# A fifth tile pair for FFN 1's second product, and residual weight parts added up by transfers

## The chip, the cores and the metric

One core of one Trainium2 chip runs the whole layer as one program. The metric is device microseconds (us) of one execution. Five engines take part, each with its own in-order instruction stream: PE (matmul), DVE (elementwise work), ACT (activation, copies), POOL (here mostly the issuer of some transfers) and SP (the issuer of most transfers). They meet through semaphores. Transfers (DMA) run on 16 DMA engines; those issued by SP appear in the profile as queue q1, those issued by POOL as queue q0.

## The reference

A layer of a streaming encoder on 512 tokens of width 1024, all in float32:

```
f = (silu(n1(x) @ w1) * (n1(x) @ w3)) @ w2          # FFN 1, D_FF = 2816 = 22 tiles of 128
h = x + 0.5 * post1(f)
... input projection, recurrent branch, windowed attention, gates, w_o: h = h + post_mix(...)
f = (silu(n2(h) @ w1') * (n2(h) @ w3')) @ w2'        # FFN 2, the same shapes
y = h + 0.5 * post2(f)
```

n1, n2 and the posts are RMS norms with a gain. The change touches the two FFNs alone.

## The kernel before

**Split operands.** Every float32 matmul is made of three: an operand is split into a high part (ACT copies it to the matmul's rounded type, `whi`) and a low part (DVE subtracts: `wlo = raw - whi`), and PE adds hi·hi, lo·hi and hi·lo. So each 128x1024 weight tile costs one ACT copy and one DVE subtraction before PE can use it.

**Pair jobs.** In the FFNs' first products (w1 and w3) two neighbouring hidden tiles make a job that needs seven quarter products in place of eight (Winograd's form of Strassen's scheme). `Pairs.run` goes through 16 such jobs for FFN 1 (hidden tiles 6 to 21, w1 and w3 in turn, two raw tiles `ra` and `rb` each) and 18 for FFN 2. The PE order in a job is: a11, s1, then the last product (a22) of the job before, then s2, a12, s4, s3. Each is one `mm_s`: four steps of three 128x256 matmuls, and ends with `point()`. While job n runs, `Pairs.prep(n + 1, i)` makes the operands of the next: i = 0 the sums S12 and S34 (DVE), i = 1 the split of `ra` (it gives a11 and a12; its low part is the `wlo<-raw_w1a` and `wlo<-raw_w3a` of the traces), i = 2 and 3 the splits of the sums, i = 4 the split of a22. ACT also copies the finished products out of PSUM in each job (q1 after a11, q5 after s1, u after s2).

**`later` and `point`.** `later(n, fn, rank)` puts work off until n calls of `point()` on; each PE product calls it. So the order on ACT, DVE, SP and POOL is set by counts of products.

**The w2 product** (`w2_gemm`) goes through 22 hidden tiles. In FFN 1 (`w2a`), `W2["w2a"] = (6, (4,), 6, 0.95)`: six tiles in the plain form, then one group of four tile pairs (tiles 6 to 13), in the form with seven products for eight, then tiles 14 and 15 plain, then the last six tiles token tile by token tile in `tok_finish`, where the norm and the residual follow. A plan sorted by due times spreads the splits and sums of all tiles ahead of PE. For FFN 2's w2 the weight parts of five pairs are made far ahead by `pre_pair` and stored in DRAM (`PRE`, `PRE_AT`); `w_load` brings them back.

**Slots.** All tiles of 128x1024 floats share 43 slots of SBUF; a load into a slot waits for the last reader of what lay there.

Of the kernel before, what the change touches and what calls it, by code (L numbers as in the profile page):

```python
# [11 lines left out]
F32R = mybir.dt.float32r  # L12
AF = mybir.ActivationFunctionType
ALU = mybir.AluOpType

P = 128
SEQ = 512
D = 1024
# [33 lines left out]
def hybrid_layer(ctx: ExitStack, tc: tile.TileContext, a: dict, out: bass.AP):  # L52
# [126 lines left out]
    def later(n, fn, rank=1):  # L179
        uid[0] += 1  # L180
        due.append((now[0] + n, rank, uid[0], fn))
# [29 lines left out]
    def unit(nm, i, **kw):  # L211
        w = get(nm, i)
        ps = bank("f")
        mm_feat(ps, w, **kw)
        return ps
# [218 lines left out]
    def pre_pair(nm, f, at0, step):  # L434
        made = PRE_TILES.setdefault(nm, {})
        dram = [tc.dram_tile([P, D], F32, name=f"pre_{nm}{f}_{i}") for i in range(5)]
        made[f] = [dram[:2], *dram[2:]]
        r, t = [], {}

        def load():  # L440
            for n in range(2):
                r.append(slot([P, D], name="rawp"))
                src = a[nm][f * P : (f + 2) * P, n * 512 : n * 512 + 512]
                sp.dma_start(out=r[n].rearrange("p (b c) -> p b c", b=2), in_=src.rearrange("(b p) c -> p b c", p=P))

        def hi(name, src, w=QH):
            if w == D:
                t[name] = slot([P, D], F32R, name="ph"), slot([P, D], F32R, name="pl")
            else:
                x = slot([P, 2, QH], F32R, name="pb")  # L450
                t[name] = x[:, 0, :], x[:, 1, :], x
            t[name] = *t[name], src
            act.activation(t[name][0], src, AF.Copy)

        def lo(name):
            x = t[name]
            dve.tensor_tensor(out=x[1], in0=x[-1], in1=f32(x[0]), op=ALU.subtract)

        def store(i, name):
            x = t.pop(name)  # L460
            if i == 0:
                for d, y in zip(dram[:2], x):
                    sp.dma_start(out=d, in_=f32(y))
            else:
                sp.dma_start(out=dram[i + 1], in_=f32(x[2].rearrange("p a b -> p (a b)")))

        def sums34():
            t34_of(*r)
            hi("t3", r[1][:, :QH])

        steps = [
            (load,),
            (),
            (lambda: hi("t12", t12_of(*r), D),),
            (lambda: lo("t12"), lambda: hi("b22", r[1][:, QH:])),
            (lambda: store(0, "t12"), lambda: lo("b22")),
            (sums34, lambda: store(1, "b22")),
            (lambda: lo("t3"), lambda: hi("t4", r[0][:, QH:])),
            (lambda: store(2, "t3"), lambda: lo("t4"), lambda: r.clear()),
            (lambda: store(3, "t4"),),  # L480
        ]
        for i, fns in enumerate(steps):
            later(at0 + i * step, lambda fns=fns: [fn() for fn in fns], 4)

    def pre_at(where):
        for nm, f, at_, step in PRE_AT.get(where, ()):
# [349 lines left out]
    QH = 4 * P  # L836
# [13 lines left out]
    class Pairs:  # L850
# [13 lines left out]
        def prep(self, m, i):  # L864
            if m >= len(self.jobs):
                return
            k = self.k0 + 2 * m
            if i == 0:
                if k not in loaded or k + 1 not in loaded:
                    self.raws(m)  # L870
                s12, s34 = slot([P, 2 * QH], name="S12"), slot([P, 2 * QH], name="S34")
                self.w[m] = {"r": (raws.pop(k), raws.pop(k + 1)), "s": (s12, s34)}
            W = self.w[m]
            (ra, rb), (s12, s34) = W["r"], W["s"]
            a11, a12, a21, a22 = ra[:, :QH], ra[:, QH:], rb[:, :QH], rb[:, QH:]

            def both(src, w=2 * QH):
                hi = slot([P, w], F32R, name="whi")
                lo = slot([P, w], F32R, name="wlo")
                split2(hi, lo, src)  # L880
                return hi, lo

            def halves(p, a, b):
                W[a] = p[0][:, :QH], p[1][:, :QH]
                W[b] = p[0][:, QH:], p[1][:, QH:]

            if i == 0:
                dve.tensor_tensor(out=s12[:, :QH], in0=a21, in1=a22, op=ALU.add)
                dve.tensor_tensor(out=s12[:, QH:], in0=s12[:, :QH], in1=a11, op=ALU.subtract)
                dve.tensor_tensor(out=s34[:, QH:], in0=a12, in1=s12[:, QH:], op=ALU.subtract)  # L890
                dve.tensor_tensor(out=s34[:, :QH], in0=a11, in1=a21, op=ALU.subtract)
            elif i == 1:
                halves(both(ra), "a11", "a12")
            elif i == 2:
                halves(both(s12), "s1", "s2")
            elif i == 3:
                halves(both(s34), "s3", "s4")
            elif i == 4:
                t = slot([P, 2, QH], F32R, name="w22")
                split2(t[:, 0, :], t[:, 1, :], a22)  # L900
                W["a22"] = t[:, 0, :], t[:, 1, :]
                del W["r"], W["s"]

        def run(self, tail, hooks={}):
# [4 lines left out]
            for n, (nm, f) in enumerate(self.jobs):  # L909
                W = self.w.pop(n)  # L910
# [7 lines left out]
                at = lambda i: [f() for f in hooks.get((n, i), ())]  # L918
                mm_s(W["a11"], X["b11"], bu)
                act.activation(q1, bu, AF.Copy)  # L920
                if n == len(self.jobs) - 1:
                    tail()
                at(1)
                mm_s(W["s1"], X["t1"], bx)
                act.activation(q5, bx, AF.Copy)
                at(2)
                last()
                self.prep(n + 1, 1)
                mm_s(W["s2"], X["t2"], bu, True)
                del W["s1"], W["s2"]  # L930
                act.activation(u, bu, AF.Copy)
# [53 lines left out]
    def load_x(k, q=sp):  # L985
        q.dma_start(out=xts[k // 2][:, k % 2, :], in_=a["xT"][k * P : (k + 1) * P, :])

    def load_w(u, kp):
        nm, i = order[u]
        c = slice(kp * 2 * P, (kp + 1) * 2 * P)  # L990
        sp.dma_start(out=raw3[u][:, c], in_=a[nm][i * P : (i + 1) * P, c])


    warm = slot([P, 512], F32R, name="warm")
# [3 lines left out]
        pe.matmul(psw, warm[:, :P], warm, start=True, stop=True)  # L998

    load_x(0, act)  # L1000
    sp.dma_start(out=vec, in_=a["vec"])
    for kp in range(KT // 2):
        load_w(0, kp)
        if kp:
            load_x(2 * kp)
        load_w(1, kp)
        load_w(2, kp)
        load_x(2 * kp + 1)
    dma_to(NS + 2)
# [54 lines left out]
    pairs_a.prep(0, 0)  # L1064
    ps.append(unit("w3a", 1))
    pairs_a.prep(0, 1)
    p1 = unit("w1a", 2)
    pairs_a.prep(0, 2)

# [19 lines left out]
    def softplus(at0, at1):  # L1089
        lam = vec[:, V_LAM : V_LAM + KT]  # L1090
        z = [small(KT, "z", 5) for _ in range(5)]

        def heads():
            act.activation(z[0], lam, AF.Abs)
            act.activation(z[1], z[0], AF.Exp, scale=-1.0)

        steps = []

        def tt(o, x, y):
            steps.append(lambda: dve.tensor_tensor(out=o, in0=x, in1=y, op=ALU.mult))  # L1100

        def ts(o, x, s1, s2, op0, op1=None):
            kw = {"op1": op1} if op1 else {}
            steps.append(lambda: dve.tensor_scalar(out=o, in0=x, scalar1=s1, scalar2=s2, op0=op0, **kw))

        ts(z[2], z[1], 2.0, None, ALU.add)
        steps.append(lambda: dve.reciprocal(z[2], z[2]))
        tt(z[1], z[1], z[2])
        tt(z[2], z[1], z[1])
        ts(z[3], z[2], 1.0 / 17, 1.0 / 15, ALU.mult, ALU.add)  # L1110
        for c in (13, 11, 9, 7, 5, 3, 1):
            tt(z[3], z[3], z[2])
            ts(z[3], z[3], 1.0 / c, None, ALU.add)
        tt(z[3], z[3], z[1])
        ts(z[4], lam, -1.0, 0.0, ALU.mult, ALU.max)
        steps.append(lambda: dve.scalar_tensor_tensor(out=z[3], in0=z[3], scalar=2.0, in1=z[4], op0=ALU.mult, op1=ALU.add))
        ts(chalf, z[3], 2.0, None, ALU.mult)
        ts(cneg, z[3], -4.0, None, ALU.mult)
        ts(bhalf, vec[:, V_BA : V_BG + 16], 0.5, None, ALU.mult)
        later(at0, heads)  # L1120
        for i, step in enumerate(steps):
            later(at1 + i, step, 4)
# [66 lines left out]
        split_to(st["split"] + 1)  # L1189

    softplus(6, 9)
    pairs_a.run(w2_ahead, late)
    X1 = pairs_a = late = None
    bs = w2_gemm("w2a", hid, "ffn1_post_g", 0.5, "mix_pre_g", [("xr", i) for i in range(4)], x_t, h1)
# [352 lines left out]
        later(2 + i, lambda i=i: X2.update({f"t{i + 1}": to_slots(tn[i])}))  # L1547
    pairs_b = Pairs("w1b", "w3b", NC2, X2, hid)
    end = 2 * 2 * (NC2 - 2)
    for i, at_ in enumerate((end - 7, end - 4, end - 3, end - 2, end - 1)):  # L1550
        later(at_, lambda i=i: pairs_b.prep(0, i))
    later(end, lambda: pairs_b.prep(1, 0))
    swiglu_units("w1b", "w3b", 2, NC2, hid)
# [17 lines left out]
SCAN_LAG = (1, 2, 3, 4, 6, 7, 9, 10)  # L1571
NSLOT = 43
RO = 6
W2 = {"w2a": (6, (4,), 6, 0.95), "w2b": (2, (4, 4), 4, 0.95)}
TR_K = {"w2a": 2, "wo": 4}
PRE = {"w2b": (2, 4, 6, 8, 14)}
PRE_AT = {"xr": [("w2b", 2, 2, 2), ("w2b", 8, 8, 2)], "xg": [("w2b", 4, 7, 1)], ("wg", 13): [("w2b", 6, 1, 1)], "wao": [("w2b", 14, 4, 1)]}
W2_LOAD = (14, 9, 8, 8)
P0A, P0B = 6, 8
W2_LEAD = 2.5  # L1580
W2_RAW = 4
W2_FLUSH = 2.5
# [57 lines left out]
```

## Time and profile before

| | |
|---|---|
| median of 3 runs | 1120.33 us (1120.18 to 1120.45) |
| profiled execution | 1120.09 us, its span 1118.3 us |
| granted TensorE clock | 0.999 |
| busy | PE 99%, DVE 81%, ACT 54%, POOL 3% of the span |
| FFN 1 pair jobs | 72.4 to 233.7 us of the span |
| FFN 1 w2, plain tiles 0 to 5 | 233.7 to 266.7 us |
| group of four pairs | 266.7 to 304.8 us |
| tiles 14 and 15 | 304.8 to 315.4 us |

The 1.8 us between span and time lie around the program. The chain of waits that ended last runs over PE for 98% of the span. Matmul records overlap, since PE is pipelined: what a matmul costs is the distance from its start to the next one's.

### The profile page before, as it was taken

The page shows a single profiled execution, that of the slowest core. Times are in us where ns is not written, and L with a number is a line of the kernel's source. Part 1 is how long each engine was busy: PE and PEld are TensorE (multiplying, and loading weights), DVE is VectorE, ACT ScalarE, POOL GpSimd, SP SyncE. Part 2 cuts the span into 40 slices and gives each one's busy share as a digit, 9 for nine tenths or more (in the row PEclk, how much of TensorE's full clock was granted, in tenths as well). Part 3 has the DMA queues.
Part 4 walks back from the last instruction along what each step waited for, and adds up shares of the span by engine and source line. Part 5 has one row for each costly group of instructions (what it writes and reads, how often), then busy time and mean ns, then how long its engine had stood idle before and what let it go on. Part 6 is the DMA issues. An engine that isn't in the chain of part 4 may idle for free.

```text
span 1118.3 us, 17215 instructions
## 1 busy us (share of the span) xinstructions
PE 1109.7 (99%) x6613; PEld 987.7 (88%) x6613; DVE 907.3 (81%) x1609; ACT 607.8 (54%) x1072; POOL 34.7 (3%) x60
## 2 busy tenths in 40 slices
PE   9999999999999999999999999999999999999997
PEld 7889999988889887888888888888999999998886
DVE  5999888888887777886799877777868888887995
ACT  7555555564455368945655664355644555555352
POOL 0000000000000000001021111000000000000000
PEclk9999999999999999999999999999999999999999
DMA  9863332260554444536232335562333322357543
GB/s 343 148 165 102 114 96 94 77 225 1 173 203 159 162 156 149 182 117 225 76 95 76 95 95 218 199 241 79 133 121 104 114 90 101 95 205 268 178 177 113
DMA packets 50482, 161.12 MB, mean 144 GB/s; under 512 B 5536, under 2 KB 7072, under 8 KB 50400
## 3 DMA queue, kind: packets, MB, share of 16 engines
q1 hardware_dynamic: 47808, 151.33, 39.3%
q0 software_dynamic: 2448, 8.43, 4.0%
q8 instruction: 52, 0.85, 0.3%
q10 hardware_dynamic: 144, 0.26, 0.1%
q14 instruction: 30, 0.25, 0.1%
HBM read 136.42 MB, written 22.54 MB: 142 GB/s over the span
## 4 chain that ended last, share of the span: by engine, by line
PE 98%; ACT 1%; DMA 1%; DVE 0%; DVEq 0%; issue 0%
PE f L205 12%; PE f L207 12%; PE f L206 12%; PE c L845 10%; PE c L847 10%; PE c L846 10%; PE acc L223 5%; PE acc L224 5%; PE acc L225 5%; PE acc L719 3%; PE acc L721 3%; PE acc L720 3%; PE pt L1446 1%; PE s L1410 1%; DMA t<-pre_w2b 1%; PE tr L294 1%
## 5 line engine op out<-in xcount | busy, mean ns | idle before, releaser
L205 PE MATMUL f<-uT,whi 128*128 128x512 f32 (+1 forms) x536 | 196.7, 367 | 0.0
L207 PE MATMUL f<-uT,whi 128*128 128x512 f32 (+1 forms) x536 | 195.2, 364 | 0.0
L206 PE MATMUL f<-uT,wlo 128*128 128x512 f32 (+1 forms) x536 | 195.1, 364 | 0.0
L205 PEld LDWEIGHTS f<-uT,whi 128*128 128x128 f32 x536 | 101.2, 189 | 16.9 <-issue 1.4
L845 PE MATMUL c<-Xh,whi 128*128 128x256 f32 x408 | 115.6, 283 | 0.1
L847 PE MATMUL c<-uT,whi 128*128 128x256 f32 x408 | 115.5, 283 | 0.0
L846 PE MATMUL c<-Xh,wlo 128*128 128x256 f32 x408 | 115.5, 283 | 0.0
L846 PE MATMUL c<-uT,wlo 128*128 128x256 f32 x408 | 115.5, 283 | 0.0
L847 PE MATMUL c<-Xl,whi 128*128 128x256 f32 x408 | 115.5, 283 | 0.0
L845 PE MATMUL c<-uT,whi 128*128 128x256 f32 x408 | 115.5, 283 | 0.0
L207 PEld LDWEIGHTS f<-uT,whi 128*128 128x128 f32 x536 | 101.1, 189 | 16.2
L206 PEld LDWEIGHTS f<-uT,wlo 128*128 128x128 f32 x536 | 101.2, 189 | 15.6
L196 DVE TENSOR_TENSOR wlo<-S,whi 128x1024 fp32r<-128x1024 f32 x68 | 82.9, 1219 | 16.4 <-ACT whi L195 16.4
L845 PEld LDWEIGHTS c<-Xh,whi 128*128 128x128 f32 x408 | 78.3, 192 | 0.3 <-ACT ct L920 0.3
L846 PEld LDWEIGHTS c<-uT,wlo 128*128 128x128 f32 x408 | 78.3, 192 | 0.0
L845 PEld LDWEIGHTS c<-uT,whi 128*128 128x128 f32 x408 | 78.3, 192 | 0.0
L846 PEld LDWEIGHTS c<-Xh,wlo 128*128 128x128 f32 x408 | 78.3, 192 | 0.0
L847 PEld LDWEIGHTS c<-uT,whi 128*128 128x128 f32 x408 | 78.3, 192 | 0.0
L847 PEld LDWEIGHTS c<-Xl,whi 128*128 128x128 f32 x408 | 78.3, 192 | 0.0
L195 ACT ACTIVATE whi<-S 128x1024 fp32r<-128x1024 f32 x68 | 68.2, 1050 | 0.0
L223 PE MATMUL acc<-whi,hT 128*128 128x512 f32 x160 | 62.5, 390 | 0.0
L224 PE MATMUL acc<-wlo,hT 128*128 128x512 f32 x160 | 62.3, 389 | 0.0
(406 smaller groups left out, 2741.6 us busy)
## 6 DMA issues: line engine op xcount, KB each, us to landing
raw_w2a<-in_w2a_dram SPq DMA_DIRECT2D x22, 512.0 KB, 4.6
raw_w1b<-in_w1b_dram SPq DMA_DIRECT2D x22, 512.0 KB, 4.5
raw_w3b<-in_w3b_dram SPq DMA_DIRECT2D x22, 512.0 KB, 4.5
raw_w3a<-in_w3a_dram SPq DMA_DIRECT2D x21, 512.0 KB, 4.2
raw_w1a<-in_w1a_dram SPq DMA_DIRECT2D x20, 512.0 KB, 4.6
raw_w2b<-in_w2b_dram SPq DMA_DIRECT2D x17, 512.0 KB, 4.1
h<-h SPq DMA_DIRECT2D x16, 512.0 KB, 3.7
raw_wg<-in_wg_dram SPq DMA_DIRECT2D x16, 512.0 KB, 3.9
```

Of the source, the lines that this page charges most:

```text
L195: act.activation(hi, src, AF.Copy)
L196: dve.tensor_tensor(out=lo, in0=src, in1=f32(hi), op=ALU.subtract)
L205: pe.matmul(ps[:, c0:c1], wh[:, s], h_, start=k == 0, stop=False)
L206: pe.matmul(ps[:, c0:c1], wl[:, s], h_, start=False, stop=False)
L207: pe.matmul(ps[:, c0:c1], wh[:, s], l_, start=False, stop=k == KT - 1)
L223: pe.matmul(acc[n], x[:, 0, c], wh[:, s], start=first, stop=False, skip_group_check=True)
L224: pe.matmul(acc[n], x[:, 0, c], wl[:, s], start=False, stop=False, skip_group_check=True)
L225: pe.matmul(acc[n], x[:, 1, c], wh[:, s], start=False, stop=last, skip_group_check=True)
L719: pe.matmul(b, h[:, c], wh, start=start and n_ == 0, stop=False, skip_group_check=True)
L845: pe.matmul(ps, wh[:, s], xh, start=first, stop=False, skip_group_check=True)
L846: pe.matmul(ps, wl[:, s], xh, start=False, stop=False, skip_group_check=True)
L847: pe.matmul(ps, wh[:, s], xl, start=False, stop=k == 3, skip_group_check=True)
```

## The change

Four edits:

1. **`W2["w2a"]` has (5,) for (4,)**: the group takes tiles 6 to 15, and no plain tiles are left between it and `tok_finish`.
2. **Pair 6's weight parts are made in the pair jobs.** `PRE["w2a"] = (6,)`; `pre_at("w1a")` before `pairs_a.run` places the steps of `pre_pair` from point 63 on (job 9 and later): two strided loads, five DVE sums, four splits, five stores of 512 KB to DRAM. In the group `w_load` reads the five back.
3. **The low part of `ra` by transfer.** From job `ADD_FROM = 3` on, in both FFNs, DVE no longer subtracts. ACT writes `wlo = -ra` in the rounded type, that is `-whi`, and POOL issues a transfer that adds `ra` onto it (`accum_op=ALU.add`, SBUF to SBUF, 512 KB). These are 13 transfers in FFN 1 and 15 in FFN 2. `prep(n + 1, 1)` (the high part) moves to right after q1 and `prep(n + 1, 5)` (the low part) stands right after q5.
4. **Start**: the first quarter of the second weight tile is loaded from ACT's queue, ahead of SP's list.

```diff
+        if nm == "w2a":
+            s = []
+            steps = [
+                (load,), (), (),
+                (lambda: s.append(slot([P, D], name="T12")), sub(...)),
...
+                (lambda: store(0, "t12"), lambda: hi("b22", r[1][:, QH:])),
...
+                (lambda: store(3, "t4"),),
+            ]
         for i, fns in enumerate(steps):
-            later(at0 + i * step, lambda fns=fns: [fn() for fn in fns], 4)
+            later(at0 + (i * step if isinstance(step, int) else step[i]), lambda fns=fns: [fn() for fn in fns], 4)
...
             elif i == 1:
-                halves(both(ra), "a11", "a12")
+                W["p"] = slot([P, 2 * QH], F32R, name="whi"), slot([P, 2 * QH], F32R, name="wlo")
+                halves(W["p"], "a11", "a12")
+                act.activation(W["p"][0], ra, AF.Copy)
+            elif i == 5:
+                hi, lo = W.pop("p")
+                if m < ADD_FROM:
+                    dve.tensor_tensor(out=lo, in0=ra, in1=f32(hi), op=ALU.subtract)
+                    return
+                act.activation(lo, ra, AF.Copy, scale=-1.0)
+                pool.dma_start(out=f32(lo), in_=ra, accum_op=ALU.add)
...
                 mm_s(W["a11"], X["b11"], bu)
                 act.activation(q1, bu, AF.Copy)
+                self.prep(n + 1, 1)
...
                 mm_s(W["s1"], X["t1"], bx)
                 act.activation(q5, bx, AF.Copy)
+                self.prep(n + 1, 5)
                 at(2)
                 last()
-                self.prep(n + 1, 1)
...
     load_x(0, act)
+    load_w(1, 0, act)
...
     softplus(6, 9)
+    pre_at("w1a")
     pairs_a.run(w2_ahead, late)
...
-W2 = {"w2a": (6, (4,), 6, 0.95), "w2b": (2, (4, 4), 4, 0.95)}
+W2 = {"w2a": (6, (5,), 6, 0.95), "w2b": (2, (4, 4), 4, 0.95)}
-PRE = {"w2b": (2, 4, 6, 8, 14)}
+PRE = {"w2a": (6,), "w2b": (2, 4, 6, 8, 14)}
+PRE_JOB = (0, 1, 2, 9, 11, 19, 21, 26, 28, 29, 33, 34, 40, 42, 43)
+ADD_FROM = 3
```

Three places where the instructions move. First POOL's stream, from the bias table's store of the start (`bias_scr`) on. Before, the next things in it are the two gain vectors of FFN 1's end (`bc_...`):

```order
L1077 DMA bias_scr<-erow_401 2048x1x383
L248 DMA bc_ffn_post_g_3349<-in_ffn_post_g_dram 128x1024
L248 DMA bc_mix_pre_g_3351<-in_mix_pre_g_dram 128x1024
L1203 DMA rgraw_3979<-in_rg_a_w_dram 64x8x64
L1203 DMA rgraw_3979<-in_rg_x_w_dram 64x8x64 x2
```

Now (the first four of the thirteen adding transfers):

```order
L1110 DMA bias_scr<-erow_401 2048x1x383
L923 DMA wlo_978<-raw_w3a_195_826 128x1024
L923 DMA wlo_1109<-raw_w1a_211_954 128x1024
L923 DMA wlo_1240<-raw_w3a_227_1085 128x1024
L923 DMA wlo_1369<-raw_w1a_243_1216 128x1024
```

POOL, idle through the pair jobs before, issues one 512 KB transfer in each from the third on, and each waits there for ACT's `wlo`.

Second, ACT in one pair job of FFN 1 (`c` is a product in PSUM, `ct` the copies q1, q5, u; `S` the sums; `w` the a22 part). Before:

```order
L920 ACTIVATE ct_1213<-c_1215 128x256
L925 ACTIVATE ct_1213<-c_1216 128x256
L195 ACTIVATE whi_1260<-raw_w3a_212_1079 128x1024
L931 ACTIVATE ct_1213<-c_1215 128x256
L195 ACTIVATE whi_1278<-S_226_1203 128x1024
L195 ACTIVATE whi_1310<-S_227_1204 128x1024
```

Now:

```order
L950 ACTIVATE ct_1220<-c_1222 128x256
L916 ACTIVATE whi_1239<-raw_w3a_227_1085 128x1024
L956 ACTIVATE ct_1220<-c_1223 128x256
L922 ACTIVATE wlo_1240<-raw_w3a_227_1085 128x1024
L962 ACTIVATE ct_1220<-c_1222 128x256
L195 ACTIVATE whi_1286<-S_241_1210 128x1024
L195 ACTIVATE whi_1318<-S_242_1211 128x1024
```

The high part has moved ahead of the q5 copy, and one copy more, `wlo`, stands behind it; the transfer that adds `ra` can start when that copy is done.

Third, DVE at the end of the group in FFN 1's w2 (`acc` are PSUM banks, `kp` kept partial results, `hT` the splits of hidden tiles, `wlo<-raw_w2a` those of weight tiles). Before, the last two banks of the group are added up with two of the eight following tiles between them, and six tiles come after:

```order
L678 TENSOR_TENSOR acc_2763<-acc_2763,kp_3179 128x512
L505 TENSOR_TENSOR hT_3205<-cc_1712,hT_3205 128x512
L505 TENSOR_TENSOR wlo_3207<-raw_w2a_581_3203,whi_3206 128x1024
L505 TENSOR_TENSOR hT_3225<-cc_1712,hT_3225 128x512
L505 TENSOR_TENSOR wlo_3227<-raw_w2a_586_3223,whi_3226 128x1024
L678 TENSOR_TENSOR acc_2765<-acc_2765,kp_3179 128x512
```

Now, with the last six tiles right behind the group:

```order
L699 TENSOR_TENSOR acc_2807<-acc_2807,kp_3306 128x512
L526 TENSOR_TENSOR hT_3371<-cc_2487,hT_3371 128x512
L526 TENSOR_TENSOR wlo_3373<-raw_w2a_641_3369,whi_3372 128x1024
L526 TENSOR_TENSOR hT_3378<-cc_2487,hT_3378 128x512
L526 TENSOR_TENSOR wlo_3380<-raw_w2a_645_3376,whi_3379 128x1024
L699 TENSOR_TENSOR acc_2809<-acc_2809,kp_3306 128x512
```

Four of these six tiles are now split before the first of the two additions; the two that stand between them are tiles 20 and 21, the last of all.

More of the change, by code (lines that the diff above doesn't have):

```diff
@@ L481, in pre_pair, with sub @@
         ]
+        def sub(o, x, y):
+            return lambda: dve.tensor_tensor(out=o(), in0=x(), in1=y(), op=ALU.subtract)
+        if nm == "w2a":
+            s = []
+            steps = [
+                (load,), (), (),
+                (lambda: s.append(slot([P, D], name="T12")), sub(lambda: s[0][:, :QH], lambda: r[1][:, :QH], lambda: r[0][:, :QH])),
+                (sub(lambda: s[0][:, QH:], lambda: r[1][:, QH:], lambda: s[0][:, :QH]),),
+                (lambda: hi("t12", s.pop(), D),),
+                (lambda: lo("t12"),),
+                (lambda: store(0, "t12"), lambda: hi("b22", r[1][:, QH:])),
+                (lambda: lo("b22"),),
+                (lambda: store(1, "b22"), sub(lambda: r[1][:, :QH], lambda: r[1][:, QH:], lambda: r[1][:, :QH])),
+                (lambda: hi("t3", r[1][:, :QH]), sub(lambda: r[0][:, QH:], lambda: r[0][:, QH:], lambda: r[0][:, :QH])),
+                (sub(lambda: r[0][:, QH:], lambda: r[0][:, QH:], lambda: r[1][:, :QH]),),
+                (lambda: hi("t4", r[0][:, QH:]), lambda: lo("t3")),
+                (lambda: store(2, "t3"), lambda: lo("t4"), lambda: r.clear()),
+                (lambda: store(3, "t4"),),
+            ]
         for i, fns in enumerate(steps):
-            later(at0 + i * step, lambda fns=fns: [fn() for fn in fns], 4)
+            later(at0 + (i * step if isinstance(step, int) else step[i]), lambda fns=fns: [fn() for fn in fns], 4)
     def pre_at(where):
@@ L986, in load_x, with load_w @@
         q.dma_start(out=xts[k // 2][:, k % 2, :], in_=a["xT"][k * P : (k + 1) * P, :])
-    def load_w(u, kp):
+    def load_w(u, kp, q=sp):
         nm, i = order[u]
         c = slice(kp * 2 * P, (kp + 1) * 2 * P)
-        sp.dma_start(out=raw3[u][:, c], in_=a[nm][i * P : (i + 1) * P, c])
+        q.dma_start(out=raw3[u][:, c], in_=a[nm][i * P : (i + 1) * P, c])
     warm = slot([P, 512], F32R, name="warm")
@@ L1005, in hybrid_layer @@
             load_x(2 * kp)
-        load_w(1, kp)
+            load_w(1, kp)
         load_w(2, kp)
@@ L1066, in hybrid_layer @@
     pairs_a.prep(0, 1)
+    pairs_a.prep(0, 5)
     p1 = unit("w1a", 2)
@@ L1549, in hybrid_layer @@
     end = 2 * 2 * (NC2 - 2)
-    for i, at_ in enumerate((end - 7, end - 4, end - 3, end - 2, end - 1)):
+    for i, at_ in enumerate((end - 7, end - 4, end - 3, end - 2, end - 1, end - 4)):
         later(at_, lambda i=i: pairs_b.prep(0, i))
@@ L1573 @@
 RO = 6
-W2 = {"w2a": (6, (4,), 6, 0.95), "w2b": (2, (4, 4), 4, 0.95)}
+W2 = {"w2a": (6, (5,), 6, 0.95), "w2b": (2, (4, 4), 4, 0.95)}
 TR_K = {"w2a": 2, "wo": 4}
-PRE = {"w2b": (2, 4, 6, 8, 14)}
-PRE_AT = {"xr": [("w2b", 2, 2, 2), ("w2b", 8, 8, 2)], "xg": [("w2b", 4, 7, 1)], ("wg", 13): [("w2b", 6, 1, 1)], "wao": [("w2b", 14, 4, 1)]}
+PRE = {"w2a": (6,), "w2b": (2, 4, 6, 8, 14)}
+PRE_JOB = (0, 1, 2, 9, 11, 19, 21, 26, 28, 29, 33, 34, 40, 42, 43)
+PRE_AT = {"w1a": [("w2a", 6, 63, PRE_JOB)], "xr": [("w2b", 2, 2, 2), ("w2b", 8, 8, 2)], "xg": [("w2b", 4, 7, 1)], ("wg", 13): [("w2b", 6, 1, 1)], "wao": [("w2b", 14, 4, 1)]}
 W2_LOAD = (14, 9, 8, 8)
 P0A, P0B = 6, 8
+ADD_FROM = 3
 W2_LEAD = 2.5
```

## The prediction

> **What bounds the kernel now.** I read the page first, then who PE waits for, then the stages around the change. Busy shares, and the chain that ended last:
>
> ```profile
> PE 1109.7 (99%) x6613; PEld 987.7 (88%) x6613; DVE 907.3 (81%) x1609; ACT 607.8 (54%) x1072; POOL 34.7 (3%) x60
> PE 98%; ACT 1%; DMA 1%; DVE 0%; DVEq 0%; issue 0%
> ```
>
> All waits of PE in the whole span (engine, line, waited for, us in total, times, longest):
>
> ```profile
> PE w L998 <- DVE warm L995: 1.5, 1, 1.5
> ```
>
> That one lies at the start. The stages by windows (length; busy PE, PEld, DVE, ACT, POOL; clock, DMA share, GB/s): pair jobs in the first two rows, then w2's plain tiles, its group, tiles 14 and 15, the finish.
>
> ```profile
> 153.00:203.00 50.00, 50.00 (x419) 50.00 (x418) 42.42 (x64) 25.55 (x41) 0.00 (x0) 1.00 0.34 107
> 203.00:233.70 30.70, 30.70 (x258) 30.70 (x258) 22.99 (x34) 20.50 (x35) 0.00 (x0) 1.00 0.38 124
> 233.70:266.40 32.70, 32.70 (x148) 27.14 (x147) 30.54 (x48) 14.95 (x23) 0.00 (x0) 1.00 0.33 109
> 266.40:304.80 38.40, 38.40 (x171) 31.76 (x171) 30.77 (x50) 18.06 (x31) 1.10 (x2) 1.00 0.35 111
> 304.80:315.40 10.60, 10.60 (x48) 8.81 (x47) 10.60 (x13) 8.78 (x12) 0.00 (x0) 1.00 1.00 360
> 315.40:350.00 34.60, 34.60 (x161) 28.61 (x160) 27.59 (x66) 16.59 (x40) 2.26 (x4) 1.00 0.33 112
> ```
>
> PE has no idle time in any of them and its clock is full. So only two things can move the end: fewer matmuls, or a new wait of PE. DVE at 42 of 50 us in the pair jobs is heavily used but ends no wait of PE; work taken off it is worth nothing by itself.
>
> **The fifth pair.** Start, duration and line of PE's matmuls in the group:
>
> ```profile
> 277.58 0.39 PE L719 MATMUL acc<-bh,uT 128*128 128x512 f32 x1
> 277.81 0.39 PE L720 MATMUL acc<-bl,uT 128*128 128x512 f32 x1
> 278.04 0.39 PE L721 MATMUL acc<-bh,uT 128*128 128x512 f32 x1
> 278.26 0.39 PE L719 MATMUL acc<-bh,uT 128*128 128x512 f32 x1
> ```
>
> The distance is 0.227 us. Tiles 14 and 15 in the plain form take 2 tiles x 4 token tiles x 2 halves x 3 = 48 matmuls (the x48 of the window 304.8 to 315.4); as a pair 7 products x 2 x 3 = 42. Six fewer are 6 x 0.227 = **-1.36 us**, all on the path. Nothing else in the change takes a matmul away.
>
> **Does DVE keep up in w2?** The last operand of the group's third product in the trace, and the seam to the finish:
>
> ```profile
> 270.41 1.23 DVE L505 TENSOR_TENSOR bl<-T,bh 128x1024 fp32r<-128x1024 f32 x1 [0.52 <-ACT bh L508]
> 302.87 0.68 DVE L505 TENSOR_TENSOR hT<-cc,hT 128x512 fp32r<-128x512 f32 x1
> 303.47 1.22 DVE L505 TENSOR_TENSOR wlo<-raw_w2a,whi 128x1024 fp32r<-128x1024 f32 x1
> 304.60 0.69 DVE L505 TENSOR_TENSOR hT<-cc,hT 128x512 fp32r<-128x512 f32 x1
> 316.23 1.22 DVE L505 TENSOR_TENSOR wlo<-raw_w2a,whi 128x1024 fp32r<-128x1024 f32 x1
> ```
>
> That operand is done at 271.6. The third product starts at 277.6 (above) and reaches its fourth pair 9 matmuls later, at 279.6: a lead of 8.0 us. Now pair 14 adds ahead of it three splits of 0.7, 0.4 and 1.2 and sums and a split of some 2.4, about 4.5 us, while its T12 only takes the place of pair 6's. DVE is done near 276.1; the product's fifth pair comes at 266.7 + 60 x 0.227 + 12 x 0.227 = 283.0, a lead of 6.9. At the seam a tile costs 1.73 (302.87 to 304.60). Tiles 20 and 21 now stand behind the addition that waits for the first t4 product, which ends 15 x 0.227 = 3.4 us ahead of the group's end; 0.6 + 2 x 1.73 later, 0.7 us after the end, tile 21 is ready, and PE wants it 15 matmuls, 3.4 us, after the end. That is a lead of 2.7 us; before it was 318.8 - 317.4 = 1.4. Both leads hold, so I cost the w2 stage at nothing. Were that cover gone, each late us would be a us.
>
> Pair 6's early work (five sums, four splits) is about 6.8 us of DVE over the seven jobs from 9 on, where seven subtractions of 1.22 = 8.5 us go. ACT gets 1.05 more per job, 5 x 1.05 on 25.6 of 50. Both stay under their stage: nothing.
>
> **The adding transfers.** This is the only new wait of PE. ACT in a pair job:
>
> ```profile
> 153.58 0.38 ACT L920 ACTIVATE ct<-c 128x256 f32<-128x256 f32 x1 [2.96 <-PE c L847]
> 155.02 0.38 ACT L925 ACTIVATE ct<-c 128x256 f32<-128x256 f32 x1 [1.06 <-PE c L847]
> 155.30 1.05 ACT L195 ACTIVATE whi<-raw_w3a 128x1024 fp32r<-128x1024 f32 x1
> 163.66 0.38 ACT L920 ACTIVATE ct<-c 128x256 f32<-128x256 f32 x1
> ```
>
> The q1 copies lie 10.08 us apart, one job; a product is a seventh, 1.44. `wlo = -ra` takes the place behind q5 that `whi` has at 155.30 and ends at 156.35, where POOL can issue. The next job's a11 starts at 163.66 - 1.44 = 162.2 and its second matmul, 0.12 later, reads `wlo`. So the transfer has **6.0 us** from issue to landing. Behind it on POOL stand only the next jobs' transfers; behind PE's wait stands everything. On DVE's old way the same operand needed 1.22.
>
> No row of before shows an accumulating transfer. The nearest (size each, median us to landing):
>
> ```profile
> BT<-bias_scr POOLq DMA_DIRECT2D x4, 128.0 KB, 2.5
> KS<-KS SPq DMA_DIRECT2D x4, 256.0 KB, 3.3
> pre_w2b<-pb SPq DMA_DIRECT2D x15, 512.0 KB, 2.9
> bc_ffn_post_g<-in_ffn_post_g_dram POOLq DMA_DIRECT2D x2, 512.0 KB, 6.1
> bc_mix_pre_g<-in_mix_pre_g_dram POOLq DMA_DIRECT2D x1, 512.0 KB, 8.2
> rawp<-in_w2b_dram SPq DMA_DIRECT2D x10, 512.0 KB, 6.2
> ```
>
> The first is of the window 559 to 562, where no load ran. And engine time, as shares of all 16 engines, in 100 to 165 us (loads) and 459 to 468.2 us (KS, SBUF to SBUF):
>
> ```profile
> q1 hardware_dynamic: 1728, 6.29, 28.7%
> q1 hardware_dynamic: 160, 0.52, 22.2%
> ```
>
> 512 KB cost 65 x 0.287 / 12 = 1.56 us as a load and 9.2 x 0.222 = 2.04 us as KS, whose rows fill half the partitions. A 128 KB issue of POOL lands in 2.5, of which 0.4 is data: 2.1 fixed. A plain copy would land in 2.1 + 1.56 = 3.7. An addition reads two operands; if that doubles the engine time, 2.1 + 3.1 = **5.2 us**, by KS's rate 2.1 + 4.1 = 6.2. The bounds are thus 3.7 and, beside loads, the 8.2 of the second gain vector. I take 5.2, since the transfer goes over all 128 partitions as the loads do: it lands 0.8 us ahead and costs nothing.
>
> The Trainium skill, DMA: Bandwidth & Descriptors, section "Anatomy of one DMA", gives 2.0 us and the bytes at 436 GB/s for a POOL-issued transfer, and Collectives: The Full Stack, section on the bandwidth ceiling, says that a reduction runs at half a copy's rate since the add needs two source reads. Together an estimate of 2.0 + 2.4 = 4.4 us, with the same outcome; no run here shows an accumulate yet.
>
> **The start.** PE leaves the warm-up when its nine matmuls are over and waits for no load after it; a load moved to another queue gives nothing, and costs nothing as long as it lands in time.
>
> **Sum.** Profiled execution 1120.09 - 1.36 = 1118.73; its own time lies 0.24 under the median of the runs. From the median: 1120.33 - 1.36 = **1119.0 us**, -0.12%. A measurement of this kernel tells about 0.2% (2.24 us) from no change, so this is "the same".
>
> **Rivals.**
> - *Late in every job (slower).* The point is 6.0 us. By the 6.1 of the gain vector on POOL's queue, the 13 + 15 = 28 transfers cost 28 x 0.1 = 2.8 us: 1121.8; by KS's 6.2, 5.6 us: 1124.6; by 6.5, 14 us: 1133; by 8.2, 28 x 2.2 = 62: 1180. For it: no row shows an accumulate, and both gain vectors are slower than 6.0. Against: those ran at DMA shares near 1.00, the pair jobs at 0.34.
> - *Late only beside loads (slower).* In the program as built, the raw loads of jobs 9 to 11 wait for slots that product s2 of the job reads last, 5.8 us into it, 1.5 us after the transfer's issue; pair 6's two strided loads (6.2 us, the slow kind) meet it in job 8. A load's 1.56 us of engine time, once or twice between the transfer's packets, puts 5.2 at 6.8 to 8.3: 0.8 to 2.3 late in four jobs, 3 to 9 us: 1122 to 1128. Against: the two loads of a job also might go behind. The Trainium skill, DMA: Bandwidth & Descriptors, section "Issuing engines are not separate DMA queues", says that transfers of all issuers interleave on the same 16 engines, which speaks for this rival.
> - *The seam.* Raw tile 21 or a gain vector comes late at the finish, whose loads lose the 10.6 us of tiles 14 and 15 (DMA share 1.00 there). 1 to 2 us eat the gain: 1120 to 1121. Against: the slots come free 6.8 us ahead of the group's end as built, not 1.6.
> - *More than the count.* PE's own rows leave nothing to gain; only the chain's 1% of ACT and DMA could, under a us. 1118.
>
> **How the numbers follow.** Hidden: 0.42, with 1119.0. Beside loads 0.25 (0.04 of it still within 0.2%), every job 0.23, seam 0.05 (within), more than 0.2% faster 0.05. So faster 0.05, same 0.42 + 0.04 + 0.05 = 0.51, slower 0.21 + 0.23 = 0.44. The range leaves out the fast tail and the every-job case above 6.5 us, under 0.2 together: 1118.3 to 1133. The likeliest case alone is 1118.5 to 1120.
>
> **What would show it.** Right: PE waits for no `wlo`; the adding transfers land in 4 to 6 us; q1 copies stay 10.08 apart in both FFNs; the group takes 47.6 us and the finish follows at once. Wrong: a wait of PE on DMA `wlo`, in all jobs from the third on or in 8 to 12 alone; or one on `wlo` of tiles 20, 21 or on a gain vector at the seam.

## The result: 1125.15 us, slower

The changed kernel takes 1125.15 us (median of 6 runs, 1123.35 to 1125.54), the kernel before beside it 1120.37 (1120.18 to 1120.45): ratio 1.004 [1.0027, 1.0053]. I had forecast 1119.0 and no measurable difference. The profiled execution took 1125.54 us, the longest of the six, with a span of 1123.7, 5.4 longer than before.

The page of the changed kernel, engines and the chain that ended last:

```profile
PE 1111.0 (99%) x6607; PEld 988.2 (88%) x6607; DVE 881.9 (78%) x1595; ACT 636.2 (57%) x1105; POOL 58.8 (5%) x88
PE 88%; DMA 4%; issue 4%; DVE 2%; ACT 1%; POOL 0%; DVEq 0%; SPq 0%; POOLq 0%; ACTq 0%
```

The six matmuls are gone (6607 for 6613) and DVE is 25 us less busy, yet PE is busy longer, and the chain now runs through transfers for 4% of the span. All waits of PE (engine, line, waited for, us in total, times, longest):

```profile
PE c L867 <- DMA wlo<-raw_w3a: 3.3, 2, 2.9
PE w L1029 <- DVE warm L1026: 1.5, 1, 1.5
PE c L867 <- DMA wlo<-raw_w3b: 0.7, 1, 0.7
```

So three waits of over 0.1 us for the low part, and one of them is most of it. PE's matmuls at these places (start, duration):

```profile
142.26 0.28 PE L866 MATMUL c<-Xh,whi 128*128 128x256 f32 x1
142.94 0.39 PE L867 MATMUL c<-Xh,wlo 128*128 128x256 f32 x1 [0.40 <-DMA wlo<-raw_w3a]
...
163.07 0.28 PE L866 MATMUL c<-Xh,whi 128*128 128x256 f32 x1
166.21 0.43 PE L867 MATMUL c<-Xh,wlo 128*128 128x256 f32 x1 [2.86 <-DMA wlo<-raw_w3a]
166.44 0.41 PE L868 MATMUL c<-Xl,whi 128*128 128x256 f32 x1
...
893.89 0.28 PE L866 MATMUL c<-uT,whi 128*128 128x256 f32 x1
894.89 0.39 PE L867 MATMUL c<-uT,wlo 128*128 128x256 f32 x1 [0.72 <-DMA wlo<-raw_w3b]
```

A second matmul is due 0.12 us behind the first, so these places lose 0.56, 3.02 and 0.88 us. And behind the long one the matmuls lie 0.21 to 0.23 apart instead of 0.12. The windows of the wait and of what follows it (columns as in the prediction; the clock is the third number from the end):

```profile
163.00:166.20 3.20, 0.35 (x3) 0.15 (x2) 2.16 (x5) 0.94 (x2) 0.00 (x0) 1.00 0.83 234
166.20:169.70 3.50, 3.49 (x17) 3.49 (x18) 1.84 (x3) 0.89 (x2) 0.00 (x0) 0.53 0.02 8
```

For 3.5 us PE ran at a granted clock of 0.53: 17 matmuls where 3.5 / 0.12 = 29 fit, 1.4 us lost. The balance is -1.36 + 0.56 + 3.02 + 0.88 + 1.4 = +4.5 of the +5.4; the rest is a matmul at half speed behind each wait (0.1 each) and smaller pieces that are not taken apart here. The wait of 3.02 and the slow clock behind it are thus most of the loss.

### The profile page after: what moved, and what is told of

Same layout as the page of the kernel before. It is cut to its first block, busy times and chain, and to the rows that moved or that the text cites. A ratio compares the mean times of both kernels' runs of the same rounds, so it can differ in the third digit from the quotient of the medians.

```text
span 1123.7 us, 17373 instructions
## 1 busy us (share of the span) xinstructions
PE 1111.0 (99%) x6607; PEld 988.2 (88%) x6607; DVE 881.9 (78%) x1595; ACT 636.2 (57%) x1105; POOL 58.8 (5%) x88
## 4 chain that ended last, share of the span: by engine, by line
PE 88%; DMA 4%; issue 4%; DVE 2%; ACT 1%; POOL 0%; DVEq 0%; SPq 0%; POOLq 0%; ACTq 0%
PE f L205 11%; PE f L207 11%; PE f L206 11%; PE c L867 8%; PE c L868 8%; PE c L866 8%; PE acc L225 4%; PE acc L223 4%; PE acc L224 4%; PE acc L741 4%; PE acc L740 4%; PE acc L742 4%; DMA raw_w3a<-in_w3a_dram 2%; DMA wlo<-raw_w3a 1%; PE pt L1480 1%
## 5 line engine op out<-in xcount | busy, mean ns | idle before, releaser
L867 PE MATMUL c<-Xh,wlo 128*128 128x256 f32 x408 | 116.6, 286 | 3.3 <-DMA wlo<-raw_w3a 3.3
L223 PE MATMUL acc<-whi,hT 128*128 128x512 f32 x144 | 56.3, 391 | 0.0
L224 PE MATMUL acc<-wlo,hT 128*128 128x512 f32 x144 | 56.1, 389 | 0.0
```

The lines of the kernel that those rows point to most:

```text
L223: pe.matmul(acc[n], x[:, 0, c], wh[:, s], start=first, stop=False, skip_group_check=True)
L224: pe.matmul(acc[n], x[:, 0, c], wl[:, s], start=False, stop=False, skip_group_check=True)
L867: pe.matmul(ps, wl[:, s], xh, start=False, stop=False, skip_group_check=True)
```

## Why the transfer came late

Three views of the DMA queues. An undisturbed transfer (window 116.9 to 121.6: queue with packets, MB, share of 16 engines; then the issue with its us to landing):

```profile
q0 software_dynamic: 144, 0.52, 56.4%
wlo<-raw_w3a POOLq DMA_DIRECT2D x1, 512.0 KB, 4.4
```

It takes 4.7 x 0.564 = 2.65 us of engine time, has its first packet about 1.4 us after its issue and lands after 4.4. Of the 28 transfers of this execution 25 landed in 4.4 to 5.6 us; the three others took 8.5, 6.3 and 6.0. The late one was issued at 157.70, two raw loads and one of pair 6's loads ahead of it. Its own row, then the queues in 158.5 to 160.8 and in 161 to 166:

```profile
wlo<-raw_w3a POOLq DMA_DIRECT2D x1, 512.0 KB, 8.5
...
q1 hardware_dynamic: 231, 0.65, 90.7%
...
q0 software_dynamic: 143, 0.52, 52.2%
q1 hardware_dynamic: 383, 0.73, 41.3%
```

Up to 160.8, 3.1 us after its issue, the late transfer has no packet at all in the second window, where SP's queue holds 91% of the engines; in the third the two share them. Of the 8.5 us, 1.8 more than usual pass before its first packet (3.2 for 1.4), and 2.3 more between its packets and to its landing.

The Trainium skill, DMA: Bandwidth & Descriptors, section "Queues, rings and completion order", says that an engine takes turns between the queues and drains a whole packet, of some 9 to 17 descriptors, before it switches. What the profile counts as packets are single pieces of at most 4 KB, 144 for such a transfer, 9 for each engine; so by that rule an engine would finish a load that it has begun before it turns to the transfer, as the empty window has it. But 112 of the window's 231 pieces are 2 KB rows, that is pair 6's loads, which had not begun when the transfer was issued and still went first. Whether the transfer's pieces were queued in time for a turn, the trace does not show.

The late one of FFN 2 (window 888.4 to 894) had no load beside it:

```profile
q0 software_dynamic: 142, 0.52, 47.3%
q8 instruction: 1, 0.02, 1.4%
wlo<-raw_w3b POOLq DMA_DIRECT2D x1, 512.0 KB, 6.3
```

One packet of instructions, 5.6 x 16 x 0.014 = 1.25 us on one of the 16 engines, and the transfer lands 1.9 us late. The short wait at 142 looks alike: its transfer (issued at 136.89, landing after 6.0) also has one packet of instructions beside it, and the nearest load is issued 3 us ahead of it. These rows show the two together; no run separates them, so the cause of the two short waits stays open.

The deadline was tighter than I had it, too. ACT's q1 copy and `wlo = -ra` of that job, and POOL's issue (start, duration):

```profile
154.63 0.39 ACT L950 ACTIVATE ct<-c 128x256 f32<-128x256 f32 x1 [2.96 <-PE c L868]
...
156.35 1.05 ACT L922 ACTIVATE wlo<-raw_w3a 128x1024 fp32r<-128x1024 f32 x1
...
157.70 0.85 POOL L923 DMA_DIRECT2D wlo<-raw_w3a  x1 [9.23 <-PE c L868]
```

ACT is done at 157.40, POOL issues 0.3 later, and the matmul that needs the data is due at 163.19: **5.5 us**, not 6.0. 8.5 less 5.5 is the wait of 3.0. (Without the wait the q1 copy of 154.63 would have had its next at 164.71, one job of 10.08 later. The product before it, started at 163.07 and taking 1.44, would have ended 0.2 ahead of that.)

## The experiments

Theory at first: the fifth pair pays its 1.36, and all that is lost is lateness of adding transfers where pair 6's strided loads meet them, and the slow clock after a long wait. The rivals: any load beside such a transfer does it; or the loss is pair 6's work and the w2 stage. The medians of all kernels (each against the kernel before beside it, 1120.37 to 1120.49):

| kernel | us | ratio, 95% |
|---|---|---|
| changed | 1125.15 | 1.0040 [1.0027, 1.0053] |
| adding transfers alone | 1131.02 | 1.0094 [1.0075, 1.0112] |
| pair alone | 1118.94 | 0.9987 [0.9978, 0.9996] |
| no early parts | 1139.03 | 1.0165 [1.0152, 1.0178] |
| job 9 by DVE | 1121.07 | 1.0005 [0.9996, 1.0013] |
| plain copy | 1120.50 | 0.9999 [0.9990, 1.0008] |
| filler | 1123.29 | 1.0024 [1.0014, 1.0034] |
| s1 first | 1125.45 | 1.0043 [1.0030, 1.0056] |
| no early parts, no adding | 1130.04 | 1.0088 [1.0075, 1.0102] |
| loads later | 1121.22 | 1.0005 [0.9996, 1.0014] |
| s1 first, inner jobs | 1120.52 | 1.0000 [0.9991, 1.0009] |
| both | 1119.06 | 0.9988 [0.9979, 0.9996] |

**The change in two halves.** Pair alone:

```diff
-ADD_FROM = 3
+ADD_FROM = 99
```

> Five pairs and pair 6's parts made in the pair jobs, but every low part by DVE as before, no adding transfer. Theory: no wait of PE is left and six matmuls are saved: 1119.0 us (1118.7 to 1119.5), 1.36 under before. Rival (DVE can't make pair 6's parts beside its own subtractions, so the relief by the transfers was needed): PE waits for DVE in the pair jobs or in w2, 1120 to 1125 us.

1118.94 us, within 0.1 of the forecast, and faster than both kernels. PE's waits:

```profile
PE w L1029 <- DVE warm L1026: 1.5, 1, 1.5
PE acc L740 <- DMA t<-pre_w2b: 1.3, 2, 1.1
```

No wait in FFN 1: DVE carries the fifth pair, pair 6's sums and all the subtractions. The short wait in FFN 2's w2 comes and goes between kernels (0.2 to 1.3 us in those that show it, none in the changed one); I did not follow it.

Adding transfers alone:

```diff
-W2 = {"w2a": (6, (5,), 6, 0.95), ...
+W2 = {"w2a": (6, (4,), 6, 0.95), ...
-PRE = {"w2a": (6,), "w2b": (2, 4, 6, 8, 14)}
+PRE = {"w2b": (2, 4, 6, 8, 14)}
-PRE_AT = {"w1a": [("w2a", 6, 63, PRE_JOB)], ...
+PRE_AT = {...
```

> The group keeps four pairs and pair 6 is not made in the pair jobs; only the adding transfers (and the order of the parts) are as changed. Theory (what costs is the meeting of one transfer with pair 6's two strided loads in job 8, the slow clock behind it, and some small meetings): without those loads the 3.0 us wait and the 1.7 us of slow clock are gone, only waits of 0 to 2 us in all stay, so 1120.4 to 1122.4 us. Rival (the adding transfers cost this much by themselves, in whatever jobs): no matmul is saved and the 6 us of waits stay, so about 1126 us.

1131.02 us, beyond both numbers, and the theory that blamed pair 6's loads alone fell, for they are not in this kernel. The two largest of PE's waits in FFN 1; then the issues on SP and on POOL in one late job of four, with the landing of its transfer:

```profile
PE c L867 <- DMA wlo<-raw_w1a: 4.1, 2, 2.7
PE c L867 <- DMA wlo<-raw_w3a: 1.9, 2, 1.3
```

```profile
203.89 0.33 SPq L142 DMA_DIRECT2D raw_w3a<-in_w3a_dram  x1
...
204.08 0.86 POOL L923 DMA_DIRECT2D wlo<-raw_w3a  x1 [10.82 <-PE c L868]
...
205.21 0.33 SPq L142 DMA_DIRECT2D raw_w3a<-in_w3a_dram  x1
...
wlo<-raw_w3a POOLq DMA_DIRECT2D x1, 512.0 KB, 7.0
```

In each of the four late jobs one raw load is issued 0.2 us ahead of the transfer; here the job's other load goes 1.1 us behind it. In the changed kernel both are issued behind it, as in this job (x2: two loads):

```profile
183.95 1.65 SPq L142 DMA_DIRECT2D raw_w3a<-in_w3a_dram  x2
...
182.70 0.86 POOL L923 DMA_DIRECT2D wlo<-raw_w3a  x1 [9.46 <-ACT wlo L922]
...
wlo<-raw_w3a POOLq DMA_DIRECT2D x1, 512.0 KB, 5.3
```

There the loads have no packet before 187.4; up to 187.1 all packets are the transfer's, 128 of 4 KB, its whole 512 KB. So ordinary loads are enough, and which side of the transfer they fall on decides. That pair 6's early work is what moved the loads of these jobs, two kernels without any adding transfer show: the first load of this kind after 160 in five pairs without the early parts, and in the pair alone, which has them:

```profile
164.78 2.46 SPq L142 DMA_DIRECT2D raw_w1a<-in_w1a_dram  x2
...
168.47 0.82 SPq L142 DMA_DIRECT2D raw_w1a<-in_w1a_dram  x2
```

They come 3.7 us later with the early parts. That this happens by shifting which buffer a load waits for is an inference.

**Job 9 by DVE.** One of the 28 transfers given back:

```diff
-                if m < ADD_FROM:
+                if m < ADD_FROM or (self.na == "w1a" and m == 9):
```

> As changed, but the low part for job 9 of FFN 1 alone is DVE's subtraction again; the strided loads stay. Theory: the wait of 3.0 us and the 1.7 us of slow clock go with this one transfer: 1125.15 - 4.7 = 1120.4 us. Rival (the backlog on the DMA engines only moves the wait to job 10's transfer): 1122 to 1124 us.

1121.07 us: one transfer cost 4.1 us, its wait and the slow clock behind it. That is 0.7 over the theory's number; three short waits for `wlo` stay in this kernel's profile (0.6, 0.4 and 0.3 us). None of them is at job 10, so the backlog did not move on to the next transfer.

**What the addition costs.** The same transfer as a plain copy:

```diff
-                pool.dma_start(out=f32(lo), in_=ra, accum_op=ALU.add)
+                pool.dma_start(out=f32(lo), in_=ra)
```

> The changed kernel with the transfer as a plain copy of the raw tile: the addition is left out, so the low parts hold the raw numbers; all else, the place of the transfer too, is unchanged. If the addition's doubled engine time (2.65 us for 512 KB, where a load needs about 1.3) is what leaves too little lead, an undisturbed transfer lands in about 3.1 us; job 9's, which stood behind two loads, in about 7.1 for 8.5, so its wait falls from 3.0 to about 1.6 us, too short to slow the clock (1.7 us), and the three short waits (0.57, 0.88, 0.15) go: 1125.2 - 1.4 - 1.7 - 1.6 = 1120.5 us. If the meeting with loads sets the landing whatever the packets cost, job 9 still waits some 3 us with the slow clock behind it: 1123.5 to 1125 us.

1120.50 us, as the theory had it. PE's wait, and an undisturbed transfer (116.6 to 120):

```profile
PE c L867 <- DMA wlo<-raw_w3a: 1.3, 1, 1.3
```

```profile
q0 software_dynamic: 144, 0.52, 37.6%
wlo<-raw_w3a POOLq DMA_DIRECT2D x1, 512.0 KB, 2.8
```

A copy takes 3.4 x 0.376 = 1.28 us of engine time and lands in 2.8; the addition doubles the engine time (2.65) and adds 1.6 us to the landing. Even the copy is late in job 9, where it lands after 6.9.

**The clock.** 24 matmuls more while PE would wait:

```diff
+                if n == 9 and self.na == "w1a":
+                    for _ in range(24):
+                        pe.matmul(full[0][:, 256:], W["a11"][0][:, :P], X["b11"](0, 0), start=True, stop=True, ...)
```

> The changed kernel with 24 matmuls more in FFN 1's job 9, ahead of its first product, on weights and a half bank that are free then; their result is not used. They fill some 2.7 of the 3.0 us in which PE waits for wlo. If the idle itself is what halves the clock afterwards, the 17 matmuls behind it run at 0.12 for 0.22 us: 1125.2 - 1.7 = 1123.4 us, and the granted clock stays near 1.00 there. If the clock drops for another reason, the slow stretch stays and the time is 1125.2 us or a little over.

1123.29 us. The same two windows as above, the wait and what follows it:

```profile
163.00:166.20 3.20, 3.08 (x26) 2.88 (x25) 2.16 (x5) 0.94 (x2) 0.00 (x0) 1.00 0.51 176
166.20:169.70 3.50, 3.50 (x30) 3.50 (x31) 1.56 (x3) 1.91 (x4) 0.00 (x0) 1.00 0.01 3
```

30 matmuls for 17, clock 1.00 for 0.53: with useless work in place of the wait the clock stayed up. So the idle of PE makes its clock fall, and a wait of 3 us costs about 4.5 (3.02 and the 1.4 behind it). The medians differ by 1.9 us, as forecast, but this is not the clock's share alone: the two intervals overlap, and the profiled execution here lacks most of the short waits too. What shows the clock's part is the windows.

The Trainium skill, TensorE: Matmul & The Clock Gate, Part 1, has the clock at half after an idle window of about 3.4 us and back after as long a busy one. The way back agrees (3.5 us). On the way there 2.9 us of waiting were enough here, and 2.7 in the kernel with adding transfers alone (clock 0.50 in the 3.0 us from 175.4 on), while the wait of 1.6 us in the inner-jobs kernel below left the clock alone (1.00 from 166.0 to 169.5, behind it).

**Pair 6's loads three products later.**

```diff
-PRE_JOB = (0, 1, 2, 9, ...
+PRE_JOB = (3, 3, 3, 9, ...
```

> The changed kernel with pair 6's two strided loads issued three products (4.3 us) later; the order of all DMAs is as it was. Job 9's transfer got its first packet 3.2 us after its issue, 1.8 later than an undisturbed one, and then shared the engines with these loads for 5.0 us instead of 2.65. If the loads already queued are what holds it, without the strided ones it lands about 1.5 to 2.5 us earlier, some 6.0 to 7.0 us after its issue: PE waits 1 us at most and the clock stays up, 1125.2 - 2.0 - 1.7 = 1121.5 us, down to 1120.5 with no wait. If the two ordinary loads ahead of them are enough (as in the kernel with four pairs, where such a transfer took 8.35), the wait stays near 3 us: 1125 us. A wait may come back at the transfer of the next job, beside which the loads now lie.

1121.22 us. The transfer of job 9, issued at 158.47 here, and what is left of waits for `wlo`:

```profile
wlo<-raw_w3a POOLq DMA_DIRECT2D x1, 512.0 KB, 5.5
```

```profile
PE c L867 <- DMA wlo<-raw_w3a: 0.9, 1, 0.9
PE c L867 <- DMA wlo<-raw_w3b: 0.5, 1, 0.5
```

It lands in 5.5 for 8.5 us, just in time; the 0.9 is the other late place, at 142. So in the changed kernel pair 6's loads did make the long wait: the raw loads still go 3.1 and 2.5 us ahead of the transfer here, and without pair 6's behind them the transfer comes in time. This is the one run that moves loads from ahead of a transfer to behind it.

**More lead.** The first two products of a job exchanged, so that a11 comes 1.44 us later:

```diff
-                mm_s(W["a11"], X["b11"], bu)
-                act.activation(q1, bu, AF.Copy)
+                mm_s(W["s1"], X["t1"], bx)
+                act.activation(q5, bx, AF.Copy)
                 self.prep(n + 1, 1)
...
-                mm_s(W["s1"], X["t1"], bx)
-                act.activation(q5, bx, AF.Copy)
+                mm_s(W["a11"], X["b11"], bu)
+                act.activation(q1, bu, AF.Copy)
```

> The changed kernel with the first two products of every pair job exchanged: s1 and then a11. The transfer is issued where it was (behind the second product), and is needed one product, 1.44 us, later: a lead of 7.4 us for 6.0. If lateness against that deadline is the whole loss, the waits of 0.57, 0.88 and 0.15 us go and job 9's falls to about 1.6 us with no slow clock behind it: 1125.2 - 1.6 - 1.4 - 1.7 = 1120.5 us. If the transfers are held by loads that PE's own products release, so that they move with it, the waits stay: 1125 us. If the s2 product now waits for the copy q1, which starts one product later, each of 36 jobs loses some 0.2 us more: 1127 us or over.

1125.45 us, and the first and the third of these hold at once. (By the deadline measured above the lead is 5.5 + 1.44 = 6.9 us, and the two FFNs have 16 + 18 = 34 jobs.)

```profile
PE c L866 <- ACT ct L956: 4.3, 5, 1.2
PE c L867 <- DMA wlo<-raw_w3a: 1.7, 1, 1.7
```

The waits for `wlo` shrank to the one I had expected; five jobs at the ends of the sequences, not all, wait for q1. So the exchange was kept only from the third job to the last but one:

```diff
+                two = [("a11", "b11", bu, q1), ("s1", "t1", bx, q5)]
+                if 2 <= n < len(self.jobs) - 1:
+                    two.reverse()
```

> The exchange of the first two products again, but not in the first two jobs and the last one of each FFN, where the s2 product had to wait for the copy q1 (4.3 us in five waits, 4.8 with what follows). The lead of the adding transfers is 7.4 us. What is left is job 9's wait of 1.7 us: 1125.45 - 4.8 = 1120.6 us. If the waits of the five jobs only hid others behind them, it is 1122 us or over.

1120.52 us, with one wait of 1.6 for `wlo` and a full clock behind it. And with pair 6's loads three products later as well:

> Both together: the lead of 7.4 us, and pair 6's loads three products later. If lateness of the transfers against a11 is all that the change loses, no wait for wlo is left and only the six matmuls count: 1119.0 us, as without adding transfers. If the transfers cost something besides (their traffic, POOL, ACT), it stays over 1120.4 us.

1119.06 us; PE's waits in full:

```profile
PE w L1031 <- DVE warm L1028: 1.5, 1, 1.5
```

The adding transfers, 28 of them, then cost nothing that this measurement tells; nor do they bring anything, for the pair alone takes 1118.94.

**Pair 6's early parts.** Five pairs, the fifth's work all in w2; with the adding transfers and without:

```diff
-PRE = {"w2a": (6,), "w2b": (2, 4, 6, 8, 14)}
+PRE = {"w2b": (2, 4, 6, 8, 14)}
```

> Five pairs and the adding transfers, but pair 6's parts are made in the w2 stage like those of the other four, with no early loads and stores. Theory: the wait in job 9 and the slow clock go, small waits of 0 to 2 us stay: 1119.0 to 1121 us, if DVE keeps up in w2. Rival (the transfers cost 6 us by themselves): about 1125 us. Rival (DVE is late in w2 with 6.8 us more work there): waits of PE on DVE in the group, 1120 to 1126 us.

> Five pairs with all of pair 6's parts made in the w2 stage, and no adding transfer (the low parts by DVE as before). The like kernel with the adding transfers took 1139.0 us, with a wait of 6.2 us for ACT in w2 and a slow clock behind it, and waits of some 5 us for wlo in the pair jobs. If pair 6's early parts are needed for w2 itself, the wait in w2 stays and only the transfers' share goes: 1129 to 1133 us. If the wait in w2 came of the transfers' lateness, it goes too, and the time is that of five pairs with the early parts, 1119 us.

1139.03 and 1130.04 us: the first lies beyond all three numbers expected of it, the second is where its first case had it. PE's waits in the second:

```profile
PE acc L740 <- ACT kp L696: 6.2, 1, 6.2
PE acc L224 <- DVE wlo L526: 1.6, 2, 0.8
```

So the early parts are needed for w2 itself: the second kernel differs from the pair alone in nothing else. ACT in that kernel, and PE at the start of the group:

```profile
255.48 1.06 ACT L529 ACTIVATE bh<-T 128x1024 fp32r<-128x1024 f32 x1 [1.21 <-DVE T L424]
...
260.93 1.06 ACT L529 ACTIVATE bh<-T 128x1024 fp32r<-128x1024 f32 x1 [1.21 <-DVE T L424]
...
270.61 1.07 ACT L696 ACTIVATE kp<-acc 128x512 f32<-128x512 f32 x2
...
273.46 0.79 PE L740 MATMUL acc<-bh,uT 128*128 128x512 f32 x1 [6.22 <-ACT kp L696]
```

Each pair takes 5.5 us of alternating DVE and ACT. One pair more is made ahead of the group, ACT's copies of the accumulators (`kp`) stand behind it in ACT's stream, and PE has waited for them since 267.2. That this order makes the wait is read from the rows.

## Where the prediction was right and wrong

- **The fifth pair, -1.36 us: right.** The pair alone came out within 0.1 us of the forecast. In the changed kernel the group's first matmul, the first one behind it and DVE's last raw tile at the seam:

```profile
272.62 0.39 PE L740 MATMUL acc<-bh,uT 128*128 128x512 f32 x1
...
320.22 0.39 PE L223 MATMUL acc<-whi,hT 128*128 128x512 f32 x1
...
320.48 1.21 DVE L526 TENSOR_TENSOR wlo<-raw_w2a,whi 128x1024 fp32r<-128x1024 f32 x1
```

  47.6 us, as worked out, and the finish follows at once. DVE is ready 1.5 us after the group's end instead of 0.7; against PE's want at 3.4 that is a lead of 1.9 for the 2.7 forecast, and it holds.
- **DVE's relief is worth nothing: right.** The pair alone has no wait of PE for DVE but the one at the start, and is as fast as the last kernel above, whose adding transfers are all in time (1118.94 and 1119.06).
- **The landing, 5.2 us: a term mis-sized, on the safe side.** Undisturbed it is 4.4; doubled engine time (2.65 for 1.28) was right. The estimate from the Trainium skill (DMA: Bandwidth & Descriptors, section "Anatomy of one DMA", with Collectives: The Full Stack, section on the bandwidth ceiling) had been 4.4, and the trace agrees.
- **The deadline, 6.0 us: mis-sized.** It is 5.5. I counted from the end of ACT's instruction, but POOL issues 0.3 later, and ACT's copy starts 0.2 behind its product's end, which I had taken as the same.
- **"It lands 0.8 us ahead and costs nothing": the step that failed.** The sum compared the landing of a transfer that has the engines to itself with the deadline, and put the 28 transfers at nothing. At job 9 the transfer landed after 8.5 us against 5.5, and PE waited 3.0. The rival of the transfer that is late only beside loads had the place (pair 6's loads, in job 8) and 2.3 us for the worst; I gave it 0.25 and took the hidden case. Part of its mechanism was missing: it put the loads between the transfer's packets, but 1.8 of the 4.1 us of delay passed before the first packet. It also had four late jobs where one was; the two short waits lie beside no load; and no case had the slow clock. That the result lies within this rival's 1122 to 1128 is in part luck. Its "against", that a job's two loads might go behind the transfer, is what happened in jobs 10 to 12. Adding transfers alone, where one load goes ahead in four jobs, took 10.5 us more than the kernel before.
- **The start, nothing: right** as far as the trace goes; no run took it apart.

The sum I should have made: a margin of 1.1 us (5.5 less 4.4) on each of 28 transfers, against a load's 1.56 us of engine time. One load just ahead uses the margin up (landings of 6.2 to 8.4 in adding transfers alone), and nothing in the order of the program keeps loads behind.

## What to carry to other kernels

A transfer on PE's path needs a lead that covers its own landing and the queue that may be ahead of it, not the landing alone; compare the margin with one neighbour's engine time before calling it hidden. Where the engine that is relieved ended no wait, handing its work to a transfer gains nothing and can lose. And in a kernel like this one price a wait of PE of 3 us at 4.5, for the clock falls behind it.

## Not expected of the hardware

- A transfer issued just behind another queue's loads did not share the engines with them from the start: no packet of it in 158.5 to 160.8, and a landing of 8.5 us for 4.4. A load issued 1.3 us behind such a transfer (at 183.95) had no packet until 187.4.
- A 16 KB packet of instructions on one engine goes with a landing 1.9 us late (6.3 for 4.4); that it is the cause is not shown.
- 2.9 us of waiting, and in another kernel 2.7, halve TensorE's clock for 3.5 us; matmuls into an unused half bank keep it up.
